# Splitting float32 weights into a rounded part and a rest: two GpSimd DMAs and one ScalarE instruction in place of casts and subtractions on the engines

## The chip, the cores and the metric

The kernel runs on one core of a Trainium2 chip. The metric is device time in microseconds (us) of one execution. Of the kernel before there are three timed runs: 1935.28, 1933.37 and 1935.31 us, median 1935.28.

## What is computed

The program is a two-layer encoder trunk on 512 tokens of width 1024, float32 throughout. Each layer is a half-step feed-forward block, a mixer and a second half-step feed-forward block:

```
x = x + 1/2 * SwiGLU_1(RMSNorm(x))            # 1024 -> 2816 -> 1024
h = RMSNorm(x); [q|k|v|u] = h @ W_in
a = windowed attention(q, k, v), |i-j| <= 128, per-head sink, relative bias
s = GLU(GELU(S5_fwd(u) + S5_bwd(u) + D*u))    # state-space part, both directions
x = x + concat(RMSNorm(a), RMSNorm(s)) @ W_out
x = x + 1/2 * SwiGLU_2(RMSNorm(x))
```

A final RMSNorm follows. All weight matrices are float32 in HBM and are used once.

## The kernel before

Channels lie on the 128 partitions and the 512 tokens on the free axis, so that every product has a 128x128 block of weights as its stationary operand and a 128x512 tile of activations as its moving one. TensorE multiplies operands of a rounded 32-bit type (`fp32r` in the trace). To keep float32 accuracy, a weight w is split into a rounded part `whi` and a rest `wlo = w - whi`, an activation likewise into `xh` and `xl`, and `mm3` (lines 214 to 218) makes three products for each block: `whi*xh`, `whi*xl`, `wlo*xh`.

The weights are laid out in HBM as 156 chunks in the order of their use (`weight_chunks`): 124 of 2048 columns (1024 KB) and 32 of 1792 columns (896 KB). A feed-forward block has three groups, of 8, 7 and 7 tiles of the inner width; a group has one "gu" chunk for each tile (gate and up projection) and then four "dn" chunks (down projection). A block thus takes 34 chunks, the four blocks 136, and the two mixers 10 each. A chunk of 2048 columns feeds 16 blocks times 3 products, 48 matmuls; one of 1792 columns feeds 42.

The path of a chunk before the change: `w_load` (lines 179 to 187) issues a DMA on SyncE's queue into one of two `raw` buffers. `w_split` (189 to 204) makes, for each half of the chunk, a ScalarE copy that rounds (line 199, `whi`) and a subtraction (line 202, `wlo`). The subtraction is VectorE's, except for 11 halves in each mixer, listed in `POOL_SPLIT`, which are GpSimd's. There are two buffers of `whi` and of `wlo`. `w_next` (206 to 212) is called where a chunk is about to be used; it has the next chunk split and two more loaded:

```
self.w_split(i + 2)
self.w_load(i + 2 + RAW_N)
```

The first chunk is split in `setup` (227 to 273) in quarters, interleaved with the loads of x.

Other work of the engines that the prediction speaks of: in a feed-forward block VectorE takes products from PSUM (382, 385, 409), ScalarE makes the SiLU and the rounded part of the activation (384, 388), and GpSimd adds the down projection to x (411). In the first feed-forward block of layer 0 and the second one of layer 0, GpSimd also makes the state-space tables of a layer (lines 701 to 704 and `cmul`), as background steps that are spread over the main work. The mixer is VectorE's, ScalarE's and GpSimd's work between many small products, with loads of tables through SyncE's queue (`s_load`, `s_load2`). A scheduler orders each engine's instructions when the program is built; an engine then takes them strictly in that order.

Of the kernel before, what the change touches and what calls it, by code (L numbers as in the profile page):

```python
# [8 lines left out]
F32 = mybir.dt.float32  # L9
F32R = mybir.dt.float32r  # L10
# [20 lines left out]
# column indices in the table of per-partition gains  # L31
# [5 lines left out]
RAW_N, W_N = 2, 2  # L37
# [3 lines left out]
# order of the parts of the token mixer (see Emit.mixer)  # L41
# [5 lines left out]
# weight chunks of the mixer, by halves, whose low parts GpSimd makes  # L47
POOL_SPLIT = {("u", 0, 0), ("u", 0, 1), ("u", 2, 0), ("q", 0, 0), ("q", 0, 1), ("q", 2, 1), ("glu", 0, 1),
              ("ws", 0, 1), ("ws", 4, 0), ("wa", 0, 1), ("wa", 4, 1)}
# low parts of q, by head of the group and half, that GpSimd makes  # L50
POOL_Q = ((2, 1), (3, 1))
# tiles of the output whose sums in the mixer VectorE makes, of the first and of the second product
ADD_V = ((0, 7), (5, 7))
# tiles of x, by first and number, as they are loaded
# [3 lines left out]
def weight_chunks():  # L58
    """Chunks of stationary blocks in the order of their use: (kind, args, columns)."""
    out = []  # L60
    for l in range(L):
        for which in (0, 1):
            if which == 1:
                out += [("u", (l, 0), 2048), ("u", (l, 2), 2048), ("kv", (l,), 2048),
                        ("q", (l, 0), 2048), ("q", (l, 2), 2048)]
                out += [("glu", (l,), 2048), ("ws", (l, 0), 2048), ("ws", (l, 4), 2048),
                        ("wa", (l, 0), 2048), ("wa", (l, 4), 2048)]
            for f0, nf in FGROUPS:
                for f in range(f0, f0 + nf):
                    out.append(("gu", (l, which, f), 2048))  # L70
                for dp in range(4):
                    out.append(("dn", (l, which, f0, nf, dp), 2 * nf * P))
    return out


class Emit:
# [83 lines left out]
    def set_bg(self, gen, steps, points):  # L160
        """Spread gen, of about so many steps, over so many points of the main work."""
        self.bg = gen
        self.bg_at, self.bg_n, self.bg_rate = 0, 0, steps / points
# [15 lines left out]
    def w_load(self, upto):  # L179
        while self.loaded < min(upto, len(self.chunks)):  # L180
            i = self.loaded
            n = self.chunks[i][2]
            t = self.sb.tile([P, CW], F32, tag="raw", bufs=RAW_N, name=f"raw{i}")
            src = self.I["w"][self.choff[i]:self.choff[i] + n * P].rearrange("(p c) -> p c", p=P)
            self.SP.dma_start(out=t[:, :n], in_=src)
            self.raw[i] = t
            self.loaded += 1

    def w_split(self, upto):
        while self.split < min(upto, len(self.chunks)):  # L190
            i = self.split
            self.w_load(i + 1)
            n = self.chunks[i][2]
            raw = self.raw.pop(i)
            hi = self.sb.tile([P, CW], F32R, tag="whi", bufs=W_N, name=f"whi{i}")
            lo = self.sb.tile([P, CW], F32R, tag="wlo", bufs=W_N, name=f"wlo{i}")
            for a in (0, n // 2):
                c = slice(a, a + n // 2)
                self.S.copy(hi[:, c], raw[:, c])  # L199
                kind, args, _ = self.chunks[i]  # L200
                eng = self.G if (kind, sum(args[1:]), int(a > 0)) in POOL_SPLIT else self.V
                eng.tensor_tensor(out=lo[:, c], in0=raw[:, c], in1=hi[:, c].bitcast(F32), op=ALU.subtract)  # L202
            self.wt[i] = (hi[:, :n], lo[:, :n])
            self.split += 1

    def w_next(self, kind):
        i = self.used
        assert self.chunks[i][0] == kind, (self.chunks[i], kind)
        self.used += 1
        self.w_split(i + 2)  # L210
        self.w_load(i + 2 + RAW_N)
        return self.wt.pop(i)
# [14 lines left out]
    def setup(self, st):  # L227
        """Constants, the input, and the first chunk of weights, in the order in which the first products want them."""
# [20 lines left out]
        raw = self.sb.tile([P, CW], F32, tag="raw", bufs=RAW_N, name="raw0")  # L249
# [8 lines left out]
        for j in range(4):  # L258
            c = slice(j * n, (j + 1) * n)
            S.copy(hi[:, c], raw[:, c])  # L260
            V.tensor_tensor(out=lo[:, c], in0=raw[:, c], in1=hi[:, c].bitcast(F32), op=ALU.subtract)
            for d in (2 * j, 2 * j + 1):
                self.x_hi(d, st)
                self.x_lo(d, st)
# [4 lines left out]
        self.loaded = self.split = 1  # L269
        SP.dma_start(out=self.ident, in_=I["ident"])  # L270
# [5 lines left out]
    def x_hi(self, d, st):  # L276
        """The rounded part of h = x * gain for tile d."""
# [6 lines left out]
    def x_lo(self, d, st):  # L284
        """The rest of h."""
# [9 lines left out]
    def x_acc(self, d, st, eng):  # L295
        """The running sum of squares."""
# [26 lines left out]
    def rstd_a(self, acc, n, w=T):  # L323
        """Column sums of acc -> 1/sqrt(mean + eps), as columns of 128 tokens."""
# [16 lines left out]
    def rstd_b(self, s, w=T):  # L341
        """The columns as one row of tokens, the same on each partition."""
# [108 lines left out]
    def cmul(self, eng, o, a, b, t, conj=False):  # L451
        """o = a * b (or conj(a) * b), pairs of (re, im)."""
# [10 lines left out]
    def exp_parts(self, x, w, R):  # L463
        """exp(x) = 2**k * (1 + em): returns (em, 2**k) as tiles of width w."""
# [19 lines left out]
    def sincos(self, th, w, R):  # L484
        """(cos(th) - 1, sin(th)) with th reduced to [-pi, pi] and then halved."""
# [32 lines left out]
    def s5_steps(self, l):  # L518
# [61 lines left out]
        # powers 0..8  # L580
# [22 lines left out]
        # input matrices, as they are and turned back by one chunk  # L603
# [15 lines left out]
        # phasors of 1, 2, 4, .. chunks, backward ones conjugate, of modulus 1  # L619
# [24 lines left out]
        # tables over the chunks, 16 groups at a time  # L644
# [36 lines left out]
        # output maps, input maps and the taps inside a chunk, 4 groups at a time  # L681
# [80 lines left out]
    def mixer(self, l, st, after):  # L762
# [6 lines left out]
        # u, with the tokens of a chunk apart: (j, c) for t = 8 c + j  # L769
# [36 lines left out]
        # state-space pieces, a quarter of the groups at a time  # L806
# [63 lines left out]
        def s_out(q):  # L870
# [16 lines left out]
            # rows (group parity, c); columns (j, group pair, channel)  # L887
# [60 lines left out]
        # attention  # L948
# [62 lines left out]
        def a_pv(n):  # L1011
# [8 lines left out]
            # rows (kv, dh); columns (head of the group, token)  # L1020
# [15 lines left out]
        # back to channels on the partitions, and the activation  # L1036
# [122 lines left out]
    def final(self, st):  # L1159
        """The last two tiles of the last product, the last norm and the output, half of the tokens at a time."""  # L1160
# [71 lines left out]
def _tiles(w, cols):  # L1232
    """w: (K, N); the 128-column blocks of w[:, cols] as [128, m, k, 128]."""
# [45 lines left out]
def _bucket(rel):  # L1279
    """Bucket of each relative distance (a constant of the shapes)."""  # L1280
# [82 lines left out]
```

## Time and profile before

| What | Value |
|---|---|
| timed runs | 1933.37, 1935.28, 1935.31 us |
| span of the profiled execution, first to last instruction | 1932.9 us |
| median run less that span | 2.4 us |
| TensorE busy | 1859.6 us, 96% of the span |
| VectorE, ScalarE, GpSimd busy | 59%, 32%, 36% |
| mean busy share of the 16 DMA engines, all queues | about 35% |
| HBM read, written | 201.11 MB, 34.75 MB |

The profile gives a span of the profiled execution and no separate device time for it; the median of the timed runs lies 2.4 us above that span. A busy share is a mean over stages that differ: the feed-forward blocks take some 1500 us of the span, the mixers the rest. A wait or a chain of waits tells which engine ended last in a stage. TensorE's clock stands in the rows as a share of its full speed: 1.00 is 2.4 GHz, 0.50 is 1.2 GHz.

### The profile page before, as it was taken

Reading aid. Unit: us, or ns where it says so; the run is one execution under the profiler, and the core shown is the slowest. Engines: PE = TensorE matmul, PEld = TensorE weight load, DVE = VectorE, ACT = ScalarE, POOL = GpSimd, SP = SyncE. Lnnn points to the kernel's source line nnn. Section 1 sums busy time; section 2 is a strip of 40 time slices with the busy share of each in tenths; the row PEclk is TensorE's granted clock in tenths of the full one; section 3 lists DMA queues with packets and bytes.
Section 4 is the critical chain, followed back from the end, with each engine's and each line's share of the span. In section 5 each row is a group of like instructions: output and inputs, shape, how many; then the busy total and the mean of one; then the engine's idle time right before and its main releaser. Section 6 shows DMA issues by size and latency. Waiting matters only on the chain. (4 is left out here: it accounts for less than half of the span.)

```text
span 1932.9 us, 23810 instructions
## 1 busy us (share of the span) xinstructions
PE 1859.6 (96%) x9416; PEld 1506.9 (78%) x9416; DVE 1138.8 (59%) x1747; ACT 627.4 (32%) x955; POOL 698.0 (36%) x586
## 2 busy tenths in 40 slices
PE   8999999996999999999999999999969999999997
PEld 6888888875667888888878888888747678888886
DVE  8645545569889634355674453436797773434435
ACT  5223223321743323223332222224227342222223
POOL 2049999235133015093483351103341330201102
PEclk9999999997999999999999999999979999999998
DMA  5533434576111233233333244424640122232321
GB/s 201 164 120 121 160 124 157 160 239 214 50 67 46 107 109 120 99 131 115 108 136 111 99 135 129 138 93 154 219 170 23 51 83 107 88 106 80 109 97 45
DMA packets 86233, 231.13 MB, mean 120 GB/s; under 512 B 31160, under 2 KB 38504, under 8 KB 70376
## 3 DMA queue, kind: packets, MB, share of 16 engines
q1 hardware_dynamic: 84888, 228.51, 35.0%
q8 instruction: 74, 1.21, 0.3%
q10 hardware_dynamic: 1232, 1.09, 0.2%
q14 instruction: 39, 0.32, 0.1%
HBM read 201.11 MB, written 34.75 MB: 122 GB/s over the span
## 5 line engine op out<-in xcount | busy, mean ns | idle before, releaser
L217 PE MATMUL psum<-blk,whi 128*128 128x512 f32 (+1 forms) x2446 | 952.9, 390 | 7.7 <-DVE blk L287 7.6
L216 PE MATMUL psum<-blk,whi 128*128 128x512 f32 (+1 forms) x2446 | 952.4, 392 | 7.5 <-ACT blk L281 6.3
L218 PE MATMUL psum<-blk,wlo 128*128 128x512 f32 (+1 forms) x2446 | 950.6, 389 | 0.9 <-DVE wlo L202 0.7
L217 PEld LDWEIGHTS psum<-blk,whi 128*128 128x128 f32 x2446 | 460.4, 188 | 106.2 <-DVE blk L287 12.8
L216 PEld LDWEIGHTS psum<-blk,whi 128*128 128x128 f32 x2446 | 460.8, 188 | 104.9 <-ACT blk L281 6.5
L218 PEld LDWEIGHTS psum<-blk,wlo 128*128 128x128 f32 x2446 | 460.3, 188 | 96.2 <-DVE wlo L202 1.1
L199 ACT CAST whi<-raw 128x1024 fp32r<-128x1024 f32 (+1 forms) x310 | 303.4, 1027 | 680.1 <-PE psum L217 466.6
L202 DVE TENSOR_TENSOR wlo<-raw,whi 128x1024 fp32r<-128x1024 f32 (+1 forms) x288 | 417.5, 1484 | 38.1 <-ACT whi L199 28.2
L385 DVE TENSOR_TENSOR blk<-psum,blk 128x512 f32<-128x512 f32 x88 | 60.6, 691 | 346.0 <-PE psum L218 343.6
L411 POOL TENSOR_TENSOR xtile<-xtile,blk 128x512 f32<-128x512 f32 x64 | 91.1, 1424 | 375.8 <-DVE blk L409 358.4
L409 DVE SCALAR_TENSOR_TENSOR blk<-psum,blk 128x512 f32<-128x512 f32 x94 | 64.9, 690 | 213.5 <-PE psum L218 203.2
L384 ACT ACTIVATE blk<-blk 128x512 f32<-128x512 f32 x88 | 55.3, 632 | 301.8 <-DVE blk L382 296.8
L701 POOL TENSOR_TENSOR blk<-blk,blk 128x512 f32<-128x512 f32 x64 | 85.4, 1346 | 92.0 <-PE psum L714 51.4
L382 DVE TENSOR_TENSOR blk<-psum,blk 128x512 f32<-128x512 f32 x88 | 60.2, 688 | 88.2 <-PE psum L218 85.4
L299 POOL TENSOR_TENSOR blk<-blk,blk 128x512 f32<-128x512 f32 x29 | 45.0, 1553 | 155.1 <-ACT blk L292 154.3
L202 POOL TENSOR_TENSOR wlo<-raw,whi 128x1024 fp32r<-128x1024 f32 x22 | 61.1, 2785 | 106.6 <-ACT whi L199 65.8
L702 POOL TENSOR_TENSOR blk<-blk,blk 128x512 f32<-128x512 f32 x64 | 85.8, 1343 | 27.5 <-PE psum L714 14.3
L704 POOL TENSOR_TENSOR blk<-blk,blk 128x512 f32<-128x512 f32 x49 | 80.2, 1642 | 2.4
L389 DVE TENSOR_TENSOR blk<-blk,blk 128x512 fp32r<-128x512 f32 x88 | 75.4, 859 | 0.7 <-ACT blk L388 0.7
L287 DVE SCALAR_TENSOR_TENSOR blk<-xtile,consts,blk 128x512 fp32r<-128x512 f32 x48 | 57.1, 1205 | 11.0 <-ACT blk L281 11.0
L1071 POOL TENSOR_TENSOR xtile<-xtile,blk 128x512 f32<-128x512 f32 x24 | 33.2, 1404 | 70.2 <-DVE blk L1069 63.7
L299 POOL TENSOR_TENSOR blk<-blk 128x512 f32<-128x512 f32 x13 | 20.5, 1574 | 99.0 <-ACT blk L292 98.8
(234 smaller groups left out, 1337.5 us busy)
## 6 DMA issues: line engine op xcount, KB each, us to landing
raw<-w SPq DMA_DIRECT2D x123, 1024.0 KB, 4.8
raw<-w SPq DMA_DIRECT2D x32, 896.0 KB, 4.6
fd<-blk SPq DMA_DIRECT2D x32, 256.0 KB, 2.8
ed<-blk SPq DMA_DIRECT2D x32, 256.0 KB, 3.4
blk<-ed SPq DMA_DIRECT2D x32, 256.0 KB, 6.3
blk<-fd SPq DMA_DIRECT2D x32, 256.0 KB, 5.2
tb<-blk SPq DMA_DIRECT2D x12, 512.0 KB, 2.9
blk<-tb SPq DMA_DIRECT2D x24, 256.0 KB, 5.8
```

The lines of the kernel that those rows point to most:

```text
L199: self.S.copy(hi[:, c], raw[:, c])
L202: eng.tensor_tensor(out=lo[:, c], in0=raw[:, c], in1=hi[:, c].bitcast(F32), op=ALU.subtract)
L216: t.matmul(out, wh, xh, start=start, stop=False)
L217: t.matmul(out, wh, xl, start=False, stop=False)
L218: t.matmul(out, wl, xh, start=False, stop=stop)
L299: eng.tensor_tensor(out=acc, in0=acc, in1=sq, op=ALU.add)
L389: V.tensor_tensor(out=lo.bitcast(F32R), in0=s, in1=hi, op=ALU.subtract)
L409: V.scalar_tensor_tensor(t, ps, 0.5, R, op0=ALU.mult, op1=ALU.mult)
L411: (V if last else self.G).tensor_tensor(out=self.x[d], in0=self.x[d], in1=t, op=ALU.add)
L701: Gp.tensor_tensor(out=full(o), in0=mat(a), in1=pwo(w, 0), op=M)
L702: Gp.tensor_tensor(out=full(t), in0=mat(b), in1=pwo(w, 1), op=M)
L704: Gp.tensor_tensor(out=o, in0=o, in1=t, op=sg)
```

## The change

The engines no longer split the weights. For each chunk:

- `w_load` issues a DMA on GpSimd's queue from the float32 weights into `whi`, whose type is the rounded one, so that the DMA casts. Behind it stands one ScalarE instruction of 2048 columns that writes `-whi` into `wlo`.
- `w_split` issues a second DMA on GpSimd's queue, from the same weights into `wlo`, which adds what it reads to what stands there.

The `raw` buffers are gone, and there are three buffers of `whi` and of `wlo` in place of two. `w_next(i)` issues the adding DMA of chunk i+1 and the casting DMA and the negation of chunk i+2. Chunk 0 is still split on the engines, from a block of the general storage; chunk 1 goes through the new path as early as `setup`. `POOL_SPLIT` is gone. All other differences are comments.

```
-RAW_N, W_N = 2, 2
+W_N = 3
...
+    def w_src(self, i):
+        n = self.chunks[i][2]
+        return self.I["w"][self.choff[i]:self.choff[i] + n * P].rearrange("(p c) -> p c", p=P)
+
     def w_load(self, upto):
         while self.loaded < min(upto, len(self.chunks)):
             i = self.loaded
             n = self.chunks[i][2]
-            t = self.sb.tile([P, CW], F32, tag="raw", bufs=RAW_N, name=f"raw{i}")
-            src = self.I["w"][self.choff[i]:self.choff[i] + n * P].rearrange("(p c) -> p c", p=P)
-            self.SP.dma_start(out=t[:, :n], in_=src)
-            self.raw[i] = t
+            hi = self.sb.tile([P, CW], F32R, tag="whi", bufs=W_N, name=f"whi{i}")
+            lo = self.sb.tile([P, CW], F32R, tag="wlo", bufs=W_N, name=f"wlo{i}")
+            self.G.dma_start(out=hi[:, :n], in_=self.w_src(i))
+            self.S.mul(lo[:, :n], hi[:, :n].bitcast(F32), -1.0)
+            self.raw[i] = (hi, lo)
             self.loaded += 1
...
-            raw = self.raw.pop(i)
-            hi = self.sb.tile([P, CW], F32R, tag="whi", bufs=W_N, name=f"whi{i}")
-            lo = self.sb.tile([P, CW], F32R, tag="wlo", bufs=W_N, name=f"wlo{i}")
-            for a in (0, n // 2):
-                c = slice(a, a + n // 2)
-                self.S.copy(hi[:, c], raw[:, c])
-                kind, args, _ = self.chunks[i]
-                eng = self.G if (kind, sum(args[1:]), int(a > 0)) in POOL_SPLIT else self.V
-                eng.tensor_tensor(out=lo[:, c], in0=raw[:, c], in1=hi[:, c].bitcast(F32), op=ALU.subtract)
+            hi, lo = self.raw.pop(i)
+            self.G.dma_start(out=lo[:, :n], in_=self.w_src(i), accum_op=ALU.add)
             self.wt[i] = (hi[:, :n], lo[:, :n])
             self.split += 1
...
         self.w_split(i + 2)
-        self.w_load(i + 2 + RAW_N)
+        self.w_load(i + 3)
...
-        raw = self.sb.tile([P, CW], F32, tag="raw", bufs=RAW_N, name="raw0")
+        raw = self.slot(4)
...
+            if j == 3:
+                self.free(raw)
...
         self.loaded = self.split = 1
+        self.w_split(2)
```

**Where the instructions stand now.** The first place is GpSimd's own order in the second feed-forward block of layer 1, first group (chunk 122 is its first; 130 to 133 are its four "dn" chunks). Before, GpSimd had only the additions to x there, and the loads stood on SyncE:

```order
L411 TENSOR_TENSOR xtile_65<-xtile_65,blk232_11435 128x512
L411 TENSOR_TENSOR xtile_65<-xtile_65,blk233_11462 128x512
L411 TENSOR_TENSOR xtile_65<-xtile_65,blk234_11497 128x512
L411 TENSOR_TENSOR xtile_65<-xtile_65,blk225_10957 128x512
L411 TENSOR_TENSOR xtile_65<-xtile_65,blk235_11558 128x512
```

The same place in the changed program (`whi130` is the rounded part of chunk 130, the number behind the underscore a buffer's serial number):

```order
L187 DMA whi130_10897<-w 128x2048
L198 DMA wlo130_10898<-w 128x2048
L187 DMA whi131_10956<-w 128x2048
L198 DMA wlo131_10957<-w 128x2048
L187 DMA whi132_11014<-w 128x2048
L198 DMA wlo132_11015<-w 128x2048
L410 TENSOR_TENSOR xtile_65<-xtile_65,blk233_11042 128x512
L187 DMA whi133_11073<-w 128x2048
L410 TENSOR_TENSOR xtile_65<-xtile_65,blk234_11069 128x512
L410 TENSOR_TENSOR xtile_65<-xtile_65,blk235_11101 128x512
L198 DMA wlo133_11074<-w 128x2048
```

The two DMAs of a chunk follow each other, and the casting DMA of the next chunk stands behind the adding DMA of this one. An adding DMA waits for the negation on ScalarE, and so does all that stands behind it.

The second place is ScalarE in the "gu" chunks just ahead of it. Before:

```order
L199 CAST whi127_11156<-raw127_11038 128x1024 x2
L388 CAST blk227_11091<-blk228_11150 128x512
L384 ACTIVATE blk229_11212<-blk229_11212 128x512
L199 CAST whi128_11219<-raw128_11100 128x1024 x2
L388 CAST blk230_11216<-blk229_11212 128x512
```

And now:

```order
L188 ACTIVATE wlo129_10840<-whi129_10839 128x2048
L383 ACTIVATE blk226_10588<-blk226_10588 128x512
L387 CAST blk231_10835<-blk226_10588 128x512
L188 ACTIVATE wlo130_10898<-whi130_10897 128x2048
L383 ACTIVATE blk226_10588<-blk226_10588 128x512
```

One negation has taken the place of two casts, and stands between the same SiLU and the same cast of activations.

The third place is GpSimd in the first feed-forward block of layer 0, among the background steps (lines 700 to 703 and 455 to 460 are the state-space tables):

```order
L198 DMA wlo18_1387<-w 128x2048
L457 TENSOR_TENSOR blk29_1216<-blk29_1216,blk24_735 128x16x32
L187 DMA whi19_1458<-w 128x1792
L703 TENSOR_TENSOR blk24_735<-blk24_735,blk36_1487 128x512
L459 TENSOR_TENSOR blk24_735<-blk17_413,blk29_1216 128x512
L701 TENSOR_TENSOR blk36_1487<-blk26_820,blk24_735 128x512
L460 TENSOR_TENSOR blk29_1216<-blk29_1216,blk24_735 128x16x32
L700 TENSOR_TENSOR blk24_735<-blk26_820,blk24_735 128x512
L703 TENSOR_TENSOR blk24_735<-blk24_735,blk36_1487 128x512
L187 DMA whi20_1527<-w 128x1792
L701 TENSOR_TENSOR blk36_1487<-blk26_820,blk24_735 128x512
L198 DMA wlo19_1459<-w 128x1792
```

Between the adding DMAs of two successive chunks stand eight tensor operations of 512 elements a partition.

## Rows read from the trace of the kernel before

**Rows 1.** Page, busy time of the engines; us, share, instructions.

```profile
PE 1859.6 (96%) x9416; PEld 1506.9 (78%) x9416; DVE 1138.8 (59%) x1747; ACT 627.4 (32%) x955; POOL 698.0 (36%) x586
```

**Rows 2.** Busy time by stretch; us, engines' busy us, clock, DMA share, GB/s.

```profile
200.00:300.00 100.00, 100.00 (x585) 82.24 (x587) 53.94 (x46) 28.08 (x41) 94.61 (x68) 1.00 0.42 140
400.00:500.00 100.00, 79.64 (x684) 65.42 (x683) 83.44 (x127) 27.63 (x52) 41.67 (x23) 0.86 0.58 189
1400.00:1500.00 100.00, 81.42 (x534) 61.33 (x532) 88.60 (x177) 48.93 (x104) 35.35 (x21) 0.86 0.28 96
1600.00:1700.00 100.00, 100.00 (x443) 82.79 (x442) 42.17 (x43) 25.36 (x30) 10.37 (x8) 1.00 0.27 95
```

**Rows 3.** ScalarE's timeline, 1690 to 1712 us; start, us, instruction, idle before.

```profile
1698.41 2.01 ACT L199 CAST whi<-raw 128x1024 fp32r<-128x1024 f32 x2 [3.83 <-PE psum L217]
...
1709.29 2.00 ACT L199 CAST whi<-raw 128x1024 fp32r<-128x1024 f32 x2 [3.83 <-PE psum L217]
```

**Rows 4.** TensorE's waits over the whole span: us in total, times, longest.

```profile
PE psum L882 <- DMA blk<-td: 17.6, 2, 9.2
PE psum L968 <- DVE blk L934: 12.1, 2, 6.9
...
PE psum L218 <- DVE wlo L202: 0.7, 1, 0.7
```

**Rows 5.** Groups of the page by line: busy us, mean ns, idle before.

```profile
L199 ACT CAST whi<-raw 128x1024 fp32r<-128x1024 f32 (+1 forms) x310 | 303.4, 1027 | 680.1 <-PE psum L217 466.6
L202 DVE TENSOR_TENSOR wlo<-raw,whi 128x1024 fp32r<-128x1024 f32 (+1 forms) x288 | 417.5, 1484 | 38.1 <-ACT whi L199 28.2
L411 POOL TENSOR_TENSOR xtile<-xtile,blk 128x512 f32<-128x512 f32 x64 | 91.1, 1424 | 375.8 <-DVE blk L409 358.4
...
L202 POOL TENSOR_TENSOR wlo<-raw,whi 128x1024 fp32r<-128x1024 f32 x22 | 61.1, 2785 | 106.6 <-ACT whi L199 65.8
```

**Rows 6.** Instructions on the tile raw: ns min, median, max, first and last start.

```profile
L199 ACT CAST whi<-raw x310: 934/1047/1060, 16.2 to 1897.8; 128x1024 fp32r<-128x1024 f32 x123, 128x896 fp32r<-128x896 f32 x32
...
L185 SPq DMA_DIRECT2D raw<-w x155: 327/328/5326, 8.9 to 1881.0; - x155
...
L260 ACT CAST whi<-raw x4: 600/602/617, 4.4 to 13.3; 128x512 fp32r<-128x512 f32 x4
```

**Rows 7.** DMA issues: count, KB each, median us from issue to landing.

```profile
raw<-w SPq DMA_DIRECT2D x123, 1024.0 KB, 4.8
...
td<-kd SPq DMA_DIRECT2D x4, 224.0 KB, 3.6
```

**Rows 8.** Busy time by stretch, 8 to 12 us, columns as in rows 2.

```profile
8.00:12.00 4.00, 3.44 (x8) 1.75 (x6) 3.73 (x4) 4.00 (x8) 2.92 (x3) 1.00 1.12 386
```

**Rows 9.** Busy time by stretch, around a gap of TensorE, columns as before.

```profile
458.00:459.00 1.00, 0.88 (x10) 0.42 (x8) 0.97 (x3) 0.00 (x0) 0.00 (x0) 1.00 0.97 393
...
461.00:462.00 1.00, 0.00 (x0) 0.00 (x0) 1.00 (x1) 0.00 (x0) 1.00 (x1) 0.87 0.10 18
462.00:463.00 1.00, 0.00 (x0) 0.00 (x0) 1.00 (x2) 0.00 (x0) 0.31 (x2) 0.50 0.79 236
...
467.00:468.00 1.00, 0.68 (x6) 0.68 (x8) 0.97 (x2) 0.95 (x3) 0.03 (x1) 0.50 0.75 238
...
472.00:473.00 1.00, 1.00 (x4) 0.60 (x4) 1.00 (x2) 0.00 (x0) 0.36 (x1) 1.00 0.96 344
```

More of the change, by code (lines that the diff above doesn't have):

```diff
@@ L46 @@
 """.split()
-POOL_SPLIT = {("u", 0, 0), ("u", 0, 1), ("u", 2, 0), ("q", 0, 0), ("q", 0, 1), ("q", 2, 1), ("glu", 0, 1),
-              ("ws", 0, 1), ("ws", 4, 0), ("wa", 0, 1), ("wa", 4, 1)}
 POOL_Q = ((2, 1), (3, 1))
```

## The prediction

> **What bounds the kernel now.** I read the busy times first. TensorE is busy for 96% of the span, and no other engine for more than 59% [rows 1]. A share over the whole span can hide stages, so the table by stretch comes next. In the middle of a feed-forward block, 1600 to 1700 us, TensorE is busy for 100.00 of 100 us with 443 matmuls at full clock, VectorE for 42 us, ScalarE for 25 and the DMA engines for 27% [rows 2]. In the mixers, 400 to 500 and 1400 to 1500 us, TensorE stands idle for 20 and 19 us and its clock falls to 0.86 on the mean [rows 2]. The third view is a timeline. One chunk's first cast follows another's by 1709.29 - 1698.41 = 10.88 us, and each time ScalarE had waited for a matmul that freed a buffer [rows 3]. The split runs ahead of TensorE and waits for it. The waits of TensorE say the same: all that it ever waited for a low part of weights from line 202 is 0.7 us, while its longest waits are the mixers', 17.6 us for a table's load and 12.1 us for a low part of q [rows 4]. So the split is off the path, and removing it from VectorE gives nothing in the feed-forward blocks. The change can gain in the mixers, and it can lose wherever its own chain takes more than 10.88 us a chunk.
>
> **What is removed.** VectorE loses 288 subtractions, 417.5 us, GpSimd 22, 61.1 us [rows 5]. All but some 88 us of that lies beside matmuls in the feed-forward blocks and is worth nothing. In the mixers, 40 half chunks, 22 of them are GpSimd's, so VectorE gets back 18 x 1.48 = 27 us there. ScalarE exchanges 310 casts for 155 negations. A cast of 512 columns takes 0.60 us and one of 1024 takes 1.05 [rows 6], so 1024 more cost about 0.9 and a negation of 2048 columns some **1.9 us**, against 2.0 for the pair: no change. SyncE's queue loses 155 loads, which can bring a table's load forward.
>
> **What is added: a loop through GpSimd's queue.** In the changed order GpSimd has cast(i), add(i), cast(i+1), add(i+1). It takes them in turn, and add(i) waits for the negation, which waits until cast(i) has landed. So cast(i+1) can't be issued before add(i), whatever buffers are free, and the time from add(i) to add(i+1) is the sum of these steps:
>
> - issue of the adding DMA. The trace has no DMA from GpSimd. SyncE's issue of a load takes 0.33 us [rows 6]; GpSimd's tensor operations on 128 partitions take 1.42 [rows 5]. I take **1.4**, the engine's own row, with 0.3 as the lower end. The casting DMA's issue lies under the adding transfer.
> - the adding transfer. A plain load of 1024 KB (1.05 MB) lands 4.8 us after its issue [rows 7]. At the most that the queues moved, 386 GB/s at a DMA share of 1.12 [rows 8], the bytes alone are 2.7 us, which leaves 2.1 for the fixed part. The adding transfer reads two streams, the weights and what stands in `wlo`, and writes one. The nearest row is two such loads, so I take **5.4**, between 2.7 (the second stream is free) and 13.7 (two streams at the pace of the slow row below).
> - the casting transfer, which shares the 16 DMA engines with the adding one just ahead of it: **2.7** after that, if the cast is free. The slow row is a table's move in smaller pieces, 224 KB in 3.6 us [rows 7]: less 2.1 fixed, 0.23 MB in 1.5 us is 153 GB/s, and 1.05 MB would take 6.9. I take 2.7 because the weights' rows of 8 KB a partition are unchanged.
> - the fixed part until it has landed, **2.1**, and the negation, **1.9**.
>
> Together 1.4 + 5.4 + 2.7 + 2.1 + 1.9 = **13.5 us** against 10.88, a loss of 2.6 us a chunk. For the 1792-column chunks the steps are 1.4 + 4.7 + 2.4 + 2.1 + 1.7 = 12.3 against 10.88 x 42/48 = 9.5, a loss of 2.8. The feed-forward blocks have 104 and 32 of them: 104 x 2.6 + 32 x 2.8 = **360 us**. TensorE would then wait for the low part at each chunk's third matmul.
>
> On the doubtful step a page has a figure. The Trainium skill, "Collectives: The Full Stack", section "The bandwidth ceiling: the fold count and why AG ≠ RS ≠ AR", says that a DMA which adds is slower than one that copies because it reads two sources, and gives 32.35 GB/s against 62.28, a ratio of 1.93. By that the adding transfer would be an estimated 5.2 us and the loss 2.4 us a chunk, some 330 us in all; no run here shows it yet.
>
> **The other terms.** Start: GpSimd issues the casting DMAs of chunks 1 and 2 at once, 2.1 MB among the first loads of x while the queues are full [rows 8]. At 386 GB/s that delays them by 5.4 us, **5**; between 0, if they lie behind x, and 10. Background steps: from 200 to 300 us GpSimd is busy for 94.61 of 100 us [rows 2], so 10.3 us a chunk, and two issues make it 13.1. That is under 13.5 and is hidden in GpSimd's waits: **0**. If the loop were faster, the cover would be gone and GpSimd itself would be late, by 13.1 - 10.9 = 2.2 us for some 16 chunks, 35 us. Mixers: the gain is at most the two waits of [rows 4], 30 us. Against it stand 20 chunks whose DMAs hold up GpSimd's sums in its queue, up to 3 us each, 60 us. Neither is visible beforehand; I take **0**. Where a late chunk holds up ScalarE at the negation, the SiLU behind it is late too, but the next matmuls don't need it for a whole chunk.
>
> The clock adds nothing by itself. In the mixer TensorE ended its work late in 458 to 459, the clock was down in 462 to 463, and after work began again in 467 to 468 it was back at full speed in 472 [rows 9]. So 3 us without work lower it, and some 4 us of half speed follow. [...] A chunk with 4 us at half speed takes 2 us more, and 12.9 still fits into 13.5.
>
> **Sum.** 1932.9 + 360 + 5 = 2298, and 2.4 around the span: **2300 us**, against a median of 1935.28. That is 19% more.
>
> **The rivals.**
>
> 1. *The adding transfer is as quick as a load, and the change gains.* If it takes 2.8 us or less, the loop is 10.9 or less, TensorE doesn't wait, and that is the point that decides. For it: DMA engines are idle for 73% of a feed-forward stretch [rows 2], and three buffers give two chunks' time, 21.8 us, from the cast to the use. Then the mixers' waits end, and the time is 1935 + 5 - 30 = 1910, or 1940 if nothing comes of them. Against it: the loop adds up to 9.7 even at the lowest end of every step, so there is hardly slack, and the background steps lose their cover. Chance **0.12**.
> 2. *The loop is near the limit.* The adding transfer takes 2.8 to 4 us, the loop 11 to 12 us: 136 x 0.1 to 1.2 us, with the 35 us of the background steps and some loss in the mixers, 1960 to 2150, say 2050. Chance **0.17**.
> 3. *Casting and adding DMAs are slow in themselves*, or are cut into small pieces, so that the change doesn't get the transfers it asks for. At 6.9 us each the loop is 1.4 + 6.9 + 6.9 + 2.1 + 1.9 = 19.2, the loss 104 x 8.3 + 32 x 7.8 = 1113 and the time 3050. Nothing in the trace excludes it, as it has no DMA that casts or adds. Chance **0.23**.
>
> **How the numbers follow.** The forecast, 2150 to 2600, has a chance of 0.48. The range leaves out most of rival 1 and the upper half of rival 3: 1960 to 2950. A measurement of this kernel tells 0.2%, 4 us, from no change. Faster by more than that: 0.07, a bit over half of rival 1. Within it: 0.03. Slower: the rest of rival 1 and all other cases, 0.90.
>
> **What would show it.** Right: in 1600 to 1700's stretch TensorE busy for about 80% instead of 100, a wait of line 214 on the DMA into `wlo` in almost every chunk, 13 to 14 us between negations, GpSimd waiting for ScalarE's line 188 ahead of the adding DMA, and DMA landings of about 10 us for `whi` and 7 to 8 for `wlo`. Wrong: TensorE still busy for 100% there (rival 1); the loop in place but the landings above 14 us (rival 3); casts issued ahead of the adding DMA's turn, so that no loop forms; or the loss in the mixers or the background steps in place of the feed-forward chunks.

## The result, and the profile after

The changed kernel takes 2196.57 us, median of four runs (2193.58 to 2199.80), against 1934.82 for the kernel before: a ratio of **1.1354**, 95% interval 1.134 to 1.1368. The forecast was slower, 2300 us, with a range of 1960 to 2950. Direction and place were right; the loss is 262 us instead of 365. The profiled execution spans 2197.7 us, 264.8 more than before.

The program's stages can be told apart in the trace by the broadcast of a norm's factor (`rstd_b`, line 345 before, 344 after). The first instruction of that line on TensorE in each stage gives these times, from one profiled execution of each kernel, here and for the experiments below as a difference to the kernel before:

| us | start | FFN1 L0 | mixer 0 | FFN2 L0 | FFN1 L1 | mixer 1 | FFN2 L1 | rest |
|---|---|---|---|---|---|---|---|---|
| before | 30.5 | 375.4 | 223.7 | 358.4 | 371.6 | 219.1 | 341.1 | 13.1 |
| after | 37.7 | 437.5 | 231.9 | 413.3 | 446.4 | 221.6 | 396.3 | 13.0 |
| after, difference | +7 | +62 | +8 | +55 | +75 | +3 | +55 | 0 |
| `e1_const` | +15 | -2 | +24 | -2 | +7 | +1 | 0 | -1 |
| `e2_copy` | +7 | +9 | -2 | -5 | +8 | -6 | 0 | 0 |
| `e3_neg512` | +7 | +55 | +9 | +67 | +72 | +11 | +72 | 0 |
| `e5_halves` | +2 | +68 | +14 | +36 | +48 | +18 | +21 | 0 |
| `e6_hi4lo2` | +5 | +51 | +34 | +11 | +32 | +8 | +3 | 0 |
| `e8_hi4lo3` | +6 | +10 | +31 | -7 | +5 | +8 | 0 | 0 |
| `e9_mix` | 0 | +4 | +5 | -1 | 0 | -2 | 0 | 0 |
| `e10_tabv` | +7 | +69 | +8 | +70 | +66 | +2 | +60 | 0 |
| `e11_halves_tabv` | +1 | +51 | +11 | +31 | +38 | +14 | +22 | 0 |

The table steps in the background run in the first three feed-forward stages, not only in the two of layer 0 (those of layer 0 last into the first block of layer 0, those of layer 1 from the second block of layer 0 into the first of layer 1). FFN2 L1 has none, so it shows the weights' path alone. The four feed-forward stages took 1446.5 us before and take 1693.5 now; they hold 247 of the 265 us.

The page's busy times, which answer to [rows 1]:

```profile
PE 1933.4 (88%) x9416; PEld 1531.4 (70%) x9416; DVE 724.1 (33%) x1459; ACT 611.7 (28%) x801; POOL 769.5 (35%) x874
```

VectorE lost 415 us of work, and the program got slower: it had not been what the program waited for. TensorE's idle time grew from 73 to 264 us. By stretch, columns as in [rows 2]:

```profile
200.00:300.00 100.00, 89.15 (x445) 71.98 (x443) 22.74 (x24) 23.13 (x25) 78.17 (x85) 0.98 0.79 203
...
500.00:600.00 100.00, 73.52 (x598) 56.33 (x597) 77.87 (x142) 39.27 (x75) 30.36 (x23) 0.86 0.60 170
1800.00:1900.00 100.00, 89.67 (x387) 71.65 (x386) 15.56 (x23) 21.87 (x20) 17.72 (x21) 1.00 0.65 164
```

In a feed-forward stretch TensorE made 443 matmuls in 100 us before [rows 2] and makes 387 now. No engine is full there, and neither are the DMA engines, at 0.65. When nothing is full, look for a chain that goes round. The waits of TensorE over the whole span (as in [rows 4]) name its end:

```profile
PE psum L214 <- DMA wlo<-w: 172.7, 94, 8.3
PE psum L835 <- DMA blk<-ud: 18.8, 2, 11.9
PE psum L881 <- DMA blk<-td: 14.8, 2, 11.5
```

The low part, for which TensorE had waited 0.7 us in all [rows 4], now costs it 172.7 us in 94 waits. The groups of the page by line (columns as in [rows 5]) close the ring:

```profile
L214 PE MATMUL psum<-blk,wlo 128*128 128x512 f32 (+1 forms) x2446 | 977.6, 402 | 172.9 <-DMA wlo<-w 172.7
...
L188 ACT ACTIVATE wlo<-whi 128x2048 fp32r<-128x2048 f32 (+1 forms) x155 | 290.0, 1871 | 1153.8 <-DMA whi<-w 1031.5
...
L198 POOL DMA_DIRECT2D wlo<-w x155 | 135.4, 873 | 1064.2 <-ACT wlo L188 980.5
...
L187 POOL DMA_DIRECT2D whi<-w x155 | 119.0, 768 | 98.0 <-PE psum L214 87.2
```

ScalarE's negation waits 1031.5 us for the casting DMA, GpSimd's adding DMA 980.5 us for the negation, and the casting DMA behind it hardly for a buffer (87.2 us). The longest waits are between the steps of the split, not between split and TensorE: before it was the other way round [rows 3].

One turn of the loop, from GpSimd's timeline (start, us, instruction, idle before it) in FFN2 L1:

```profile
2027.78 0.87 POOL L198 DMA_DIRECT2D wlo<-w  x1 [6.66 <-ACT wlo L188]
2028.38 0.84 POOL L187 DMA_DIRECT2D whi<-w  x1
2028.94 2.84 POOL L410 TENSOR_TENSOR xtile<-xtile,blk 128x512 f32<-128x512 f32 x2
2039.77 0.86 POOL L198 DMA_DIRECT2D wlo<-w  x1 [7.99 <-ACT wlo L188]
```

and from ScalarE's in the same stretch:

```profile
2037.56 1.92 ACT L188 ACTIVATE wlo<-whi 128x2048 fp32r<-128x2048 f32 x1 [10.07 <-DMA whi<-w]
```

The busy times microsecond by microsecond (last two columns: share of the DMA engines, GB/s) show what the DMA engines do in that turn:

```profile
2028.00:2029.00 1.00, 1.00 (x6) 0.84 (x5) 0.37 (x1) 0.00 (x0) 1.00 (x3) 1.00 0.00 0
2029.00:2030.00 1.00, 1.00 (x7) 0.81 (x6) 0.00 (x0) 0.00 (x0) 1.00 (x2) 1.00 1.02 115
2030.00:2031.00 1.00, 1.00 (x6) 0.84 (x5) 0.00 (x0) 0.00 (x0) 1.00 (x2) 1.00 0.68 115
2031.00:2032.00 1.00, 1.00 (x6) 0.82 (x5) 0.00 (x0) 0.00 (x0) 0.78 (x1) 1.00 1.11 229
2032.00:2033.00 1.00, 0.86 (x4) 0.38 (x2) 0.56 (x1) 0.00 (x0) 0.00 (x0) 1.00 1.08 222
2033.00:2034.00 1.00, 0.00 (x0) 0.00 (x0) 0.13 (x1) 0.00 (x0) 0.00 (x0) 1.00 1.04 215
2034.00:2035.00 1.00, 0.00 (x0) 0.00 (x0) 0.00 (x0) 0.00 (x0) 0.00 (x0) 1.00 0.94 349
2035.00:2036.00 1.00, 0.97 (x4) 0.84 (x5) 0.00 (x0) 0.00 (x0) 0.00 (x0) 1.00 1.00 401
2036.00:2037.00 1.00, 1.00 (x6) 0.79 (x6) 0.00 (x0) 0.00 (x0) 0.00 (x0) 1.00 0.87 336
2037.00:2038.00 1.00, 1.00 (x6) 0.85 (x5) 0.00 (x0) 0.44 (x1) 0.00 (x0) 1.00 0.00 0
```

These rows count a packet in the microsecond in which it starts; the trace's records of single packets (here one partition's row of a chunk) are finer. After the issue at 2027.78 the first packet of the adding transfer, of a 1792-column chunk, starts at 2029.36, and its last one ends at 2034.67; under way, with the engines full, it moves 215 to 229 GB/s. The casting transfer of the next chunk runs from 2034.25 to 2037.13, at about 400 GB/s in its fullest row. TensorE stops at 2032.86 for want of the low part and goes on at 2035.03, when it has landed. The negation starts at 2037.56, when the cast has landed, takes 1.92, and the next adding DMA is issued at 2039.77. From one adding DMA to the next: 11.99 us; for two 2048-column chunks in a row (2039.77 to 2052.37) 12.6. From 2037.13 to that next issue no weights move.

### The profile page after: what moved, and what is told of

Same layout as the page of the kernel before. It is cut to its first block, busy times and chain, and to the rows that moved or that the text cites. A ratio compares the mean times of both kernels' runs of the same rounds, so it can differ in the third digit from the quotient of the medians.

```text
span 2197.7 us, 23688 instructions
## 1 busy us (share of the span) xinstructions
PE 1933.4 (88%) x9416; PEld 1531.4 (70%) x9416; DVE 724.1 (33%) x1459; ACT 611.7 (28%) x801; POOL 769.5 (35%) x874
## 4 chain that ended last, share of the span: by engine, by line
issue 30%; DMA 16%; PE 13%; POOL 9%; DVE 4%; ACT 3%; SPq 0%; POOLq 0%; DVEq 0%; ACTq 0%
DMA whi<-w 8%; DMA wlo<-w 5%; PE psum L214 3%; PE psum L212 3%; PE psum L213 3%; POOL whi L187 2%; POOL xtile L410 2%; ACT wlo L188 2%; POOL wlo L198 2%; DMA blk<-ud 1%; POOL blk L298 1%; PE psum L1000 1%; PE psum L968 1%; POOL blk L700 1%; DMA ed<-blk 1%
## 5 line engine op out<-in xcount | busy, mean ns | idle before, releaser
L214 PE MATMUL psum<-blk,wlo 128*128 128x512 f32 (+1 forms) x2446 | 977.6, 402 | 172.9 <-DMA wlo<-w 172.7
L212 PE MATMUL psum<-blk,whi 128*128 128x512 f32 (+1 forms) x2446 | 974.7, 400 | 17.4 <-ACT blk L280 11.3
L213 PE MATMUL psum<-blk,whi 128*128 128x512 f32 (+1 forms) x2446 | 971.0, 397 | 9.7 <-DVE blk L286 7.3
L188 ACT ACTIVATE wlo<-whi 128x2048 fp32r<-128x2048 f32 (+1 forms) x155 | 290.0, 1871 | 1153.8 <-DMA whi<-w 1031.5
L212 PEld LDWEIGHTS psum<-blk,whi 128*128 128x128 f32 x2446 | 472.4, 193 | 121.8 <-ACT blk L280 13.2
L213 PEld LDWEIGHTS psum<-blk,whi 128*128 128x128 f32 x2446 | 471.2, 193 | 114.8 <-DVE blk L286 12.7
L198 POOL DMA_DIRECT2D wlo<-w x155 | 135.4, 873 | 1064.2 <-ACT wlo L188 980.5
L187 POOL DMA_DIRECT2D whi<-w x155 | 119.0, 768 | 98.0 <-PE psum L214 87.2
L388 DVE TENSOR_TENSOR blk<-blk,blk 128x512 fp32r<-128x512 f32 x88 | 87.3, 994 | 133.5 <-ACT blk L387 133.2
L700 POOL TENSOR_TENSOR blk<-blk,blk 128x512 f32<-128x512 f32 x64 | 76.8, 1260 | 35.6 <-DMA ed<-blk 25.8
L701 POOL TENSOR_TENSOR blk<-blk,blk 128x512 f32<-128x512 f32 x64 | 79.8, 1262 | 16.6 <-DMA ed<-blk 13.1
L387 ACT CAST blk<-blk 128x512 fp32r<-128x512 f32 x88 | 54.2, 617 | 68.8 <-DVE blk L384 67.0
L703 POOL TENSOR_TENSOR blk<-blk,blk 128x512 f32<-128x512 f32 x49 | 69.3, 1440 | 1.0
L280 ACT ACTIVATE blk<-xtile,consts 128x512 fp32r<-128x512 f32 x48 | 34.0, 715 | 53.4 <-DVE xtile L410 27.1
```

The lines of the kernel that those rows point to most:

```text
L187: self.G.dma_start(out=hi[:, :n], in_=self.w_src(i))
L188: self.S.mul(lo[:, :n], hi[:, :n].bitcast(F32), -1.0)
L198: self.G.dma_start(out=lo[:, :n], in_=self.w_src(i), accum_op=ALU.add)
L212: t.matmul(out, wh, xh, start=start, stop=False)
L213: t.matmul(out, wh, xl, start=False, stop=False)
L214: t.matmul(out, wl, xh, start=False, stop=stop)
```

## The experiments

All but one start from the changed kernel, and ratios are to the kernel before, run on the same chip. The theory: one ordered ring (adding DMA, casting DMA of the next chunk, landing, negation, adding DMA) sets the pace. The rivals: the 16 DMA engines can't move a second read of all weights beside the rest, GpSimd is too busy, or the mixers lose it.

**`e1_const`: cut the ring at ScalarE.**

```
-            self.S.mul(lo[:, :n], hi[:, :n].bitcast(F32), -1.0)
+            self.S.mul(lo[:, :n], self.ones.to_broadcast([P, n]), -1.0)
```

> Edit: the ScalarE instruction writes a constant (-1) into the low part in place of the negative of the rounded part, so it no longer waits for the casting DMA; both DMAs, their order on GpSimd's queue and ScalarE's 2048 columns a chunk stay. The low part comes out as w - 1, so the output isn't the reference's. Loop theory (GpSimd's queue holds the next cast behind an adding DMA that waits for cast, landing and negation, 12.6 us a chunk): the loop is cut, the two transfers take about 4.9 + 2.6 = 7.5 us of DMA time a chunk, under TensorE's 10.9, so the feed-forward loss ends: 1945 to 1980 us. Rival, bandwidth (317 MB through the adding and casting queue is too much for the 16 DMA engines): the bytes are the same, 2150 to 2200 us. Rival, GpSimd's time (two issues of 0.8 us a chunk and its own sums): also unchanged, 2150 to 2200 us.

Measured: 1975.98 us, ratio 1.0205 (1.019 to 1.0221). The same DMAs with the same bytes, the same instructions on GpSimd and ScalarE; only the negation doesn't wait for the cast. By stretch, and GpSimd's waits over the span:

```profile
1700.00:1800.00 100.00, 100.00 (x443) 82.81 (x442) 16.61 (x24) 23.63 (x21) 20.64 (x25) 1.00 0.78 193
```

```profile
POOL whi L187 <- PE psum L214: 690.7, 111, 31.5
POOL wlo L198 <- ACT wlo L188: 128.1, 82, 4.7
```

TensorE is full again, at a higher DMA share (0.78) than the changed kernel's 0.65, and GpSimd now waits for TensorE to free a buffer, as ScalarE did before [rows 3]. So neither the bandwidth nor GpSimd's time set the loss; the ring did. The feed-forward stages together are within 3 us of those of the kernel before; the 40 that remain are the start and the first mixer.

**`e2_copy`: the second DMA copies and doesn't add.**

```
-            self.G.dma_start(out=lo[:, :n], in_=self.w_src(i), accum_op=ALU.add)
+            self.G.dma_start(out=lo[:, :n], in_=self.w_src(i))
```

> Edit: the second DMA writes the weights over the low part and doesn't add; everything waits as before. The low part comes out as w, so the output isn't the reference's. Loop theory: the adding transfer of about 4.9 us becomes one of 2.6, the loop 12.6 - 2.3 = 10.3 us, just under TensorE's 10.9: 1955 to 2010 us. Rival, bandwidth: also faster, as a third of the queue's work goes, 2000 to 2060 us. Rival, GpSimd's time: the issues are the same, 2150 to 2200 us.

Measured: 1945.87 us, ratio 1.0056 (1.0039 to 1.0073), some 9 us under what was expected. The ring is as before, every wait in place, but shorter. DMA issues (count, KB each, median us to landing), and a stretch:

```profile
whi<-w POOLq DMA_DIRECT2D x123, 1024.0 KB, 6.8
wlo<-w POOLq DMA_DIRECT2D x123, 1024.0 KB, 5.2
```

```profile
1700.00:1800.00 100.00, 100.00 (x443) 82.81 (x442) 18.00 (x26) 24.36 (x23) 16.08 (x24) 1.00 0.57 198
```

The changed kernel has there

```profile
whi<-w POOLq DMA_DIRECT2D x123, 1024.0 KB, 9.7
wlo<-w POOLq DMA_DIRECT2D x123, 1024.0 KB, 7.9
```

The adding costs 2.7 us a chunk over a cast from the same place. Without it the ring fits under TensorE's 10.88 us [rows 3]. Both halves of the theory are thus shown: the ring and the slow adding transfer are each necessary.

**`e3_neg512`: lengthen one step of the ring**, by a second negation of 512 columns, some 0.6 us.

```
             self.S.mul(lo[:, :n], hi[:, :n].bitcast(F32), -1.0)
+            self.S.mul(lo[:, :512], hi[:, :512].bitcast(F32), -1.0)
```

> Edit: ScalarE negates the first 512 columns of each chunk a second time, some 0.6 us more between the landing of the cast and the adding DMA; the output is the same. Loop theory: every chunk whose loop is the bound gets 0.6 us longer, about 110 to 136 of them: 65 to 80 us more, 2260 to 2280 us. Rivals, bandwidth and GpSimd's time: ScalarE is busy for 28% and no DMA changes, so no change, 2190 to 2200 us.

Measured: 2231.82 us, ratio 1.153 (1.1513 to 1.1547): 35 us more than the changed kernel, half of what was expected. FFN2 L1, without tables, takes 17 us more, 0.5 us for each of its 34 chunks, as the theory has it, and FFN2 L0 12; but FFN1 L0 and FFN1 L1 take 7 and 3 less. Why is not settled; with tables in the background a longer step of the ring does not simply add up to a longer stage.

**`e5_halves`: the same work in two halves,** so that the second half's cast lies beside the first half's negation, and so on.

```
-            self.G.dma_start(out=hi[:, :n], in_=self.w_src(i))
-            self.S.mul(lo[:, :n], hi[:, :n].bitcast(F32), -1.0)
+            for a in (0, n // 2):
+                c = slice(a, a + n // 2)
+                self.G.dma_start(out=hi[:, c], in_=self.w_src(i)[:, c])
+            for a in (0, n // 2):
+                c = slice(a, a + n // 2)
+                self.S.mul(lo[:, c], hi[:, c].bitcast(F32), -1.0)
...
+            for a in (0, n // 2):
+                c = slice(a, a + n // 2)
+                self.G.dma_start(out=lo[:, c], in_=self.w_src(i)[:, c], accum_op=ALU.add)
```

> Edit: the changed kernel with each chunk cast, negated and added in two halves of 1024 columns, on the same three buffers and in the same order on GpSimd's queue; the output is the same. Loop theory: the first negation waits for half a cast (1.3 us sooner) and takes half as long (0.9 us sooner), and the first adding transfer covers the second negation, so the loop falls from 12.6 to about 10.4 us, below TensorE's 10.9, and the second feed-forward block of layer 1 takes about 341 us as before in place of 396. GpSimd's background stretches pay for two more issues a chunk: 1950 to 2050 us in all. Rival, slow transfers as such: the bytes are the same and the pieces smaller, 2190 us or more.

Measured: 2141.55 us, ratio 1.1079 (1.1046 to 1.1111), a miss. FFN2 L1 lost 21 us instead of 55, and TensorE is nearly full there:

```profile
1800.00:1900.00 100.00, 95.62 (x408) 76.93 (x408) 14.85 (x22) 21.66 (x25) 33.90 (x41) 0.98 0.79 181
```

But FFN1 L0 lost 68, more than the 62 of the changed kernel. Four DMA issues a chunk took GpSimd 508 us in place of 254, and the tables are on GpSimd too. Whether that was the cause is tried below.

**`e6_hi4lo2` and `e8_hi4lo3`: take the ring apart.** Four buffers of `whi`, the cast three chunks ahead, the negation next to the adding DMA instead of next to the cast. `e6_hi4lo2` has two buffers of `wlo`; `e8_hi4lo3` has three, with the adding DMA one chunk earlier (`w_split(i + 3)`) and one block less of general storage (15 of 16).

```
+            hi = self.sb.tile([P, CW], F32R, tag="whi", bufs=4, name=f"whi{i}")
             self.G.dma_start(out=hi[:, :n], in_=self.w_src(i))
-            self.S.mul(lo[:, :n], hi[:, :n].bitcast(F32), -1.0)
...
+            lo = self.sb.tile([P, CW], F32R, tag="wlo", bufs=2, name=f"wlo{i}")
+            self.S.mul(lo[:, :n], hi[:, :n].bitcast(F32), -1.0)
             self.G.dma_start(out=lo[:, :n], in_=self.w_src(i), accum_op=ALU.add)
...
-        self.w_split(i + 2)
-        self.w_load(i + 3)
+        self.w_load(i + 4)
+        self.w_split(i + 2)
```

> Edit: four buffers of the rounded part and two of the low part in place of three each, the cast issued three chunks ahead and the negation moved to just ahead of the adding DMA, so that on GpSimd's queue a cast stands two chunks ahead of the adding DMA that needs it; the output is the same. Loop theory: an adding DMA no longer waits for a cast just issued; cast and adding DMA of different chunks start together when TensorE frees a buffer, 2.6 + 4.9 + 2.9 = 10.4 us to the low part's landing, within one chunk of 10.9: 1945 to 2000 us. Rival, bandwidth or GpSimd's time: the same DMAs and issues, 2150 to 2200 us.

Measured: 2072.53 us, ratio 1.0708 (1.0664 to 1.0751), a miss. Where no tables run the loss is gone, FFN2 L1 at +3 us; a stretch of it, then one with tables, and TensorE's wait over the span:

```profile
1800.00:1900.00 100.00, 100.00 (x442) 82.80 (x442) 16.61 (x24) 23.88 (x21) 20.86 (x25) 1.00 0.78 192
```

```profile
200.00:300.00 100.00, 92.34 (x481) 73.34 (x480) 20.57 (x25) 23.67 (x27) 80.58 (x81) 0.97 0.81 203
```

```profile
PE psum L214 <- DMA wlo<-w: 67.0, 37, 7.5
```

With two buffers a low part can be begun only when its buffer comes free, one chunk ahead of its use: 1.9 for the negation and 8 to 9 for the landing, in 10.88. There is no slack for a transfer that the tables' loads and stores delay.

> Edit: as e6_hi4lo2 with three buffers of the low part in place of two and the negation and the adding DMA one chunk earlier, paid for with one block of the general storage (15 in place of 16); the output is the same. Theory of the second limit (in e6 a low part is started when its buffer comes free, one chunk ahead, and its landing of 8.3 us in clear stretches and up to 16.6 beside the table traffic has no slack left in 10.9): the start comes one chunk sooner and the feed-forward blocks lose nothing, 1945 to 1985 us. Rival, bandwidth beside the tables (the DMA engines are full there and late whatever the start): the first block of layer 0 stays some 50 us and the first of layer 1 some 30 us above the kernel before, 2050 to 2080 us.

Measured: 1986.70 us, ratio 1.0266 (1.0249 to 1.0284), just above the expected range; the rival's 2050 to 2080 falls. TensorE's wait for the low part is 3.2 us over the whole span:

```profile
PE psum L214 <- DMA wlo<-w: 3.2, 2, 1.7
```

and the four feed-forward stages take 8 us more than before in sum. The second cause is thus shown: with the ring gone, it is lookahead for the low part that the stages with tables need. Most of what remains, 31 us, is the first mixer. There GpSimd's queue stands at a casting DMA whose buffer isn't free, with the mixer's own sums behind it. GpSimd's waits in that stage:

```profile
POOL whi L186 <- PE psum L214: 67.5, 5, 30.1
```

The same wait was 30.1 us in the changed kernel's first mixer (+8 us), 32.4 in `e2_copy` (-2), 86.1 in `e1_const` (+24) and 109.0 in `e6_hi4lo2` (+34). That the two go together is measured; that the one makes the other is argued, as no run took the wait away alone.

**`e9_mix`: only where VectorE is busy.** From the kernel before: three weight chunks of each mixer ("glu" and "ws") go through the two DMAs, all others are split as before.

```
+            if self.chunks[i][0] in ("glu", "ws"):
+                self.loaded += 1
+                continue
...
+                self.G.dma_start(out=hi[:, :n], in_=src)
+                self.S.mul(lo[:, :n], hi[:, :n].bitcast(F32), -1.0)
+                self.G.dma_start(out=lo[:, :n], in_=src, accum_op=ALU.add)
```

> Edit: the kernel before, with its two buffers, and the DMA split for three chunks of each mixer alone (the gate's and the two of the first output product), all of it issued where the chunk would have been split; the output is the same. It asks whether the mixers gain where VectorE is the busiest engine: VectorE loses 3 half chunks of 1.5 us and GpSimd 3 of 2.8 in each. If they gain, 1927 to 1933 us. Rival: the chain of about 20 us (cast, negation, adding DMA) holds up GpSimd's sums and comes late, 1940 to 1960 us. No change would be 1934.

Measured: 1939.87 us, ratio 1.0022 (1.0013 to 1.0031): no gain, about 0.2% lost. Mixer 1 gained 2 us, mixer 0 lost 5, FFN1 L0 4. TensorE's longest waits in sum are for two instructions with which VectorE makes q in the mixer:

```profile
PE psum L979 <- DVE blk L945: 12.8, 2, 7.2
PE psum L979 <- DVE blk L941: 10.1, 2, 7.1
```

In the kernel before the first was 12.1 us [rows 4] and the second

```profile
PE psum L968 <- DVE blk L930: 3.5, 2, 2.4
```

so the freed time did not bring q forward.

**`e10_tabv` and `e11_halves_tabv`: GpSimd without the tables.** The tables' tensor operations go to VectorE, in the changed kernel and in `e5_halves`.

```
-        V, S, Gp, SP, TE, dr = self.V, self.S, self.G, self.SP, self.T, self.dram
+        V, S, Gp, SP, TE, dr = self.V, self.S, self.V, self.SP, self.T, self.dram
```

> The changed kernel with the state-space tables' tensor operations given to VectorE, so that in the feed-forward blocks GpSimd's queue holds little but the two DMAs of a chunk and the additions to x. Nothing is left out. The stages with tables lost 62 us (first block of layer 0), 55 (second of layer 0) and 75 (first of layer 1), the one without tables 55 (second of layer 1). Theory, GpSimd's own steps between an adding DMA and the next casting DMA lengthen the loop: the first blocks come down to about 50 to 58 lost, the total to 2165 to 2185 us. Rival, what the tables cost there is their own DMA traffic (moves through HBM beside the weights' two reads) or waits for their data: no change, 2190 to 2203. If VectorE becomes late with its products: above 2203.

Measured: 2220.76 us, ratio 1.1472 (1.1455 to 1.1489). The theory of this run falls: with GpSimd's steps gone the three stages with tables lost 205 us in place of 192. Who waited for the casting DMA in the first 470 us, in the changed kernel and then in this one, shows why:

```profile
  ACT wlo L188: 226.8, 28
```

```profile
  ACT wlo L188: 247.2, 26
```

What GpSimd no longer does, ScalarE waits for the cast instead; the cast landed in a median of 9.4 us there, and now in 10.6. An earlier issue only puts it sooner into the line behind the adding transfer. From one adding DMA to the next it is a median of 13.4 us in FFN1 L0 in both kernels. So GpSimd's steps did lie under the transfers. That what the tables add is in the transfers is argued from this; no run took the tables' traffic away. The run is even 24 us slower than the changed kernel by the medians and 18 by the profiled executions, 15 of these in FFN2 L0; that is not settled. VectorE had 45.72 us of work in 200 to 300 us, so it wasn't full.

> The same move of the tables' operations to VectorE, in the kernel that casts, negates and adds each chunk in two halves. There the stage without tables lost only 21 us, those with tables still 63, 36 and 48. Theory, GpSimd's own steps (twice as many DMA issues, and tensor operations between them) are what the halves could not shorten: each of the three falls towards 20 to 35 lost, total 2060 to 2100 us. Rival, the tables' DMA traffic: 2130 to 2150.

Measured: 2109.30 us, ratio 1.0905 (1.0886 to 1.0923), 9 us above the expected range. With four issues a chunk and a shorter ring, GpSimd's steps are no longer covered: the three stages lost 120 us in place of 152 (the 63 for FFN1 L0 in the expectation counts 5 us of that stage to the start; the table has 68). The rest, 9 to 29 us a stage over FFN2 L1's 22, may be the tables' transfers; it was not taken apart further.

No version was faster than the kernel before. Four buffers of both parts, which would take a further block of the general storage, were not tried; nor was `e8_hi4lo3`'s order in the feed-forward blocks with the engines' split in the mixers, which at best equals a TensorE that was full already.

## Why the prediction was right, and where its sizes were off

**The ring: right.** `e1_const` cut it and the loss in the feed-forward stages went. The signs that were named are there, two of them weaker than foretold: TensorE below 100% with waits of line 214 on the DMA into `wlo`, GpSimd waiting at the adding DMA for line 188, landings of 9.7 and 7.9 us for the foretold 10 and 7 to 8. TensorE was 90% busy, not 80, and waited for `wlo` 92 times in the 136 feed-forward chunks, not in almost every one.

**Its length: 12.0 to 12.6 us, not 13.5.** For the turn shown above, an adding transfer of 1792 and a casting one of 2048 columns, the prediction's terms are:

| step | predicted | measured |
|---|---|---|
| issue of the adding DMA until its first packet, and from the cast's last packet until the negation | 1.4 + 2.1 | 1.6 + 0.4 |
| adding and casting transfer | 4.7 + 2.7 | 7.8 |
| negation, and until the next adding DMA is issued | 1.9 | 2.2 |
| sum | 12.8 | 12.0 |

For two chunks of 2048 columns in a row the transfers take 8.4 us for the foretold 8.1, and the turn 12.6 for 13.5. The mis-sized term is the issue and the fixed part, 3.5 for 2.0: GpSimd holds its queue for 0.87 us at such an issue, not for the 1.4 of its tensor operations [rows 5], and a load's 4.8 us to landing [rows 7] holds the time from its issue to its first bytes already, so that was counted twice. The transfers, on which the rivals turned, were sized well (386 GB/s was not the most that the queues moved, as [rows 9] has 393 in one microsecond, but that shifts no term by 0.1 us). In the rows above casting and adding stand at 401 to 222 GB/s, a ratio of 1.8; single packets of 8192 bytes took a median of 0.629 us when they add, in FFN2 L1, and 0.325 when they only cast, in the same stage of `e2_copy`, a ratio of 1.94. The Trainium skill's "Collectives: The Full Stack" (section "The bandwidth ceiling: the fold count and why AG ≠ RS ≠ AR") has the ratio 1.93 between a collective whose transfers copy and one whose transfers add. The trace agrees with it.

**The loss: 247 us, not 360.** With 12.6 against 10.88 for 104 chunks, and about 11.5 against 9.5 for 32, the same formula gives 104 x 1.7 + 32 x 2.0 = 241. That it comes so close is partly luck: it gives each stage 60, where FFN2 L1 lost 55 and the three with tables 62, 55 and 75.

**Background steps, priced at nothing: the reason held, the price didn't.** `e10_tabv` shows that GpSimd's steps were covered. But the stages with tables lost 62, 55 and 75 us where the one without lost 55, 27 more together, and the median turn of the ring is 13.4 us in FFN1 L0 against 12.6 in FFN2 L1. The tables' own transfers, which the prediction left out, share the DMA engines: a move of a table that landed in 3.6 us [rows 7] now takes 9.0. That these transfers are the 27 us is likely and not shown.

```profile
td<-kd SPq DMA_DIRECT2D x4, 224.0 KB, 9.0
```

**Start +7 for 5, mixers +11 for 0:** both within what was allowed. VectorE's freed time in the mixers is worth little: with transfers that don't add (`e2_copy`) the mixers are 8 us shorter than before, with three split chunks each (`e9_mix`) 3 longer.

**The clock "adds nothing": mostly right, as far as it was tried.** In the four feed-forward stages TensorE is idle for 177.5 us more than before and busy for 69.5 us more with nearly the same matmuls; that is the 247. (In FFN2 L1 alone it is busy for 354.7 us in place of 339.2, with 1541 matmuls both times, at a mean granted clock of 0.98 in place of 1.00.) In the four stages together the clock stood at half speed for 106 us more than before, which accounts for at most 53 of the 69.5; the rest is open. That the slower matmuls aren't a cost of their own is argued: the ring above closes without TensorE in it, and a slower TensorE only waits less. No run held the clock.

**The rivals.** The quick adding transfer falls by its rate, the slow casting and adding transfers by the 400 and 222 GB/s. The forecast's own range, 2150 to 2600, holds the result near its lower end, next to the rival of a loop near the limit.

## What to carry to other kernels

Work moved from an engine with time to spare gains nothing, and the chain that does it instead has to be added up as a ring: if two dependent DMAs share one in-order queue with a compute step between them, the next chunk can't start before this one is through, and more buffers alone, which no run tried, have little to give: the casting DMA hardly waited for one here (87.2 us). What helped was another order of issue together with more buffers (`e8_hi4lo3`). Add the ring's steps up against the time of the consumer; here a DMA share of 65% beside a TensorE that waits was its mark. When the ring is cut, ask how far ahead the last step runs, since without slack any other transfer ends up on the path.

## What the hardware showed that was not expected

A DMA that casts 32-bit floats into the rounded type costs next to nothing over a plain load: its packets of 8192 bytes took a median of 0.325 us in FFN2 L1 of `e2_copy`, those of the plain loads 0.309 in the same stage of the kernel before. One that adds took 0.629 for a packet, and ran at 215 to 229 GB/s with the DMA engines full.

Gaps of the same length leave TensorE's clock alone or not. After the one shown above, 2032.86 to 2035.03 (2.2 us), it stayed at 1.00. After another of 2.2 us in the same stage it was halved, from 2.4 to 1.2 GHz, for about 3 us, beginning more than a microsecond after the work went on (the clock is the third column from the right):

```profile
2071.00:2072.00 1.00, 0.46 (x3) 0.04 (x1) 0.00 (x0) 0.00 (x0) 0.00 (x0) 1.00 1.10 229
2072.00:2073.00 1.00, 0.00 (x0) 0.00 (x0) 0.00 (x0) 0.00 (x0) 0.00 (x0) 1.00 0.82 197
2073.00:2074.00 1.00, 0.38 (x2) 0.34 (x3) 0.00 (x0) 0.00 (x0) 0.00 (x0) 1.00 1.01 401
2074.00:2075.00 1.00, 1.00 (x6) 0.82 (x5) 0.00 (x0) 0.00 (x0) 0.00 (x0) 0.96 1.16 467
2075.00:2076.00 1.00, 1.00 (x4) 0.81 (x3) 0.00 (x0) 0.00 (x0) 0.00 (x0) 0.50 0.39 139
...
2078.00:2079.00 1.00, 1.00 (x6) 0.77 (x5) 0.34 (x1) 0.62 (x2) 0.60 (x2) 0.83 0.00 0
```

The prediction had taken from [rows 9] that 3 us without work lower the clock. Here 2.2 us came before a fall in one case and not in the other, so these rows do not let one tell from a gap's length alone whether the clock will fall.
